# Two-layer hybrid decoder trunk: alternating half-array products, norms by a mean matrix, and a float32 output projection for half of the mixer

## The chip, the cores and the metric

The kernel runs on one core of a Trainium2 chip, as one launch. The metric is device time in microseconds (us). In the profile the engines are PE (TensorE matmuls), PEld (TensorE weight loads), DVE (VectorE), ACT (ScalarE), POOL (GpSimd) and SP (SyncE, which issues most transfers).

## The reference

Two layers act on x (1 x 256 x 1024, float32). Each layer is a half-step SwiGLU feed-forward block, a mixer, and a second half-step SwiGLU block; every one is preceded by an RMS norm and a modulation (shift, scale, gate) that comes from `silu(c) @ ada_w`. The mixer multiplies the normalized x by one matrix of 3088 columns and gives the columns to three groups:

- 8 attention heads of width 64, with normalized and rotated queries and keys, causal over 256 positions (one block, so plain causal attention);
- a convolution group of 256 channels: gate, causal depthwise convolution of 31 taps, a layer norm over each group of 64 channels, silu;
- 4 heads of gated linear attention, in chunks of 64 positions, with a log decay from a rank-16 gate, an RMS norm over each head's 64 values, and a silu gate.

```python
proj = h @ mix_w_in[l]
a_q, a_k, a_v, b_u, c_q, c_k, c_v, c_r, c_g = jnp.split(proj, splits, axis=-1)
o_b = _conformer_conv(b_u, conv_w[l], conv_b[l], conv_norm_g[l], conv_norm_b[l])
log_decay = jax.nn.log_sigmoid(c_g @ gla_gate_w[l] + gla_gate_b[l]) / GLA_TAU
o_c = _merge_heads(_rmsnorm(o_c, gla_out_norm[l])) * jax.nn.silu(c_r)
mixed = jnp.concatenate([o_a, o_b, o_c], axis=-1) @ mix_w_out[l]
x = x + gt2[:, None, :] * mixed
```

## The kernel before

Everything stays on chip, transposed: features on the 128 partitions, the 256 positions along the free axis. x is eight tiles of 128 x 256 (`xT`).

**Products with weights.** Each weight piece of 1 MB is fetched to a `raw` buffer (five of them, `fetch`), and `split` makes two float32r tiles of it: ACT casts a high part `wh` (L328) and DVE subtracts it for a low part `wl` (L331). The other operand is split in the same way (`hT`, `g`, `mix`). A product is then three float32r matmuls, high by high, high by low and low by high (L350 to L352, L356 and L357, L707 to L709, and in the output projection L959 to L961). The small products of the mixer, and the transposes, are float32 without a split, in banks named `tp`.

**The mixer** (`mix`). Its line of work is: convolution inputs first (the 31 taps, L741, then run on DVE between other work), the gate product (L775, L781), then q, k and v in three projections of 512 columns. `attend` is called for four pairs of heads: scores (L838; one head of the pair lies on partitions 0 to 63, the other on 64 to 127), masked maximum on DVE (L845), exponent on ACT, reciprocal of the sum on DVE (L855), scaling on ACT, three transposes on PE (L860), a copy, and the products with v (L865, L866; each head writes one half of the output's partitions). Between the pairs lie the projections of the linear attention. Its own small products are pA (L900, masked into `acaus` by DVE at L905), pS (L916), the running state S on DVE (L921, L926), and pO (L933 with `acaus`, L938 with S).

**The group norms.** `group_rstd` serves the linear attention's output and the convolution's: sums of squares by a matmul with a two-column matrix `grp` (L667), so that the result is 128 x 8; the reciprocal root on that small tile (`rsqrt`: L372, L377 to L386), and eight matmuls with the identity that spread each column over 64 partitions (L674). The convolution also subtracts a mean, which a matmul with the block matrix `grpb` gives (L746).

**The output projection** runs over four pieces of two 128-row blocks, in the order 0, 2 (attention), 6 (linear attention), 4 (convolution). The outputs of all three groups are split (`split_out`, L679 and L680) and multiplied as above.

**What sets the order.** A tile scheduler orders the instructions of each engine before the run, from the program's order, its dependencies and its buffers. At run time every engine works through its own list in that fixed order, and waits on semaphores. The modulation (`ada`, L225 on PE or L234 on DVE, summed at L253 and transposed at L265) is spread over the rest.

Of the kernel before, what the change touches and what calls it, by code (L numbers as in the profile page):

```python
# [17 lines left out]
P = 128  # L18
# [41 lines left out]
def trunk_kernel(ctx: ExitStack, tc: tile.TileContext, x, c, positions, ada_w, ada_b, ffn1_norm, ffn1_w_in,  # L60
# [43 lines left out]
    POOL.memset(epsc, EPS)  # L104
    hpi = keep([P, 1], F32, "hpi")
    POOL.memset(hpi, 1.5707963267948966)

    grp = keep([P, 2], F32, "grp")
    POOL.memset(grp, 0.0)
    POOL.memset(grp[0:64, 0:1], 1.0 / 64)  # L110
    POOL.memset(grp[64:128, 1:2], 1.0 / 64)
# [48 lines left out]
    gatew = keep([32, T], F32, "gatew")  # L160
# [48 lines left out]
    def ada_steps(l):  # L209


        for m0, n in ada_groups(l):
            width = 32 * n
            per = 16 // n
            acc = part = None
            for k in range(KD):
                if k % per == 0:
                    raw = ada_ahead.pop(0) if ada_ahead else next(ada_raws)
                w = raw[:, k % per]
                if ada_mode[0] == "pe":  # L220
                    first = acc is None
                    if first:
                        acc = bank()
                    for q in range(4):
                        PE.matmul(acc[32 * q:32 * q + 32, 0:width], cact[:, k, :], w[:, q, :], start=first,  # L225
                                  stop=(k == KD - 1 and part is None), tile_position=(0, 32 * q))
# [78 lines left out]


# [7 lines left out]
    def split(src, shape, fine=False, raw=None, between=lambda n: None):  # L314
# [23 lines left out]

        state["piece"] += 1
# [6 lines left out]
        return view(hs), view(ls)  # L346
# [336 lines left out]
    def mix(l, done):  # L683
# [31 lines left out]
        for j in range(2):  # L715
            nc.sync.dma_start(gatew[16 * j:16 * j + 16, :], gla_gate_w[l])
# [14 lines left out]
        def conv_steps():  # L731

            y = tv
            for k in range(CK):
                for t in range(2):
                    w = cw[l][:, 2 * k + t:2 * k + t + 1]
                    if k == 0:
                        DVE.tensor_scalar(y[:, t, :], hpad[:, t, 0:T], w, cols[l][:, R_CB + t:R_CB + t + 1],
                                          op0=ALU.mult, op1=ALU.add)
                    else:  # L740
                        DVE.scalar_tensor_tensor(y[:, t, :], hpad[:, t, k:k + T], w, y[:, t, :], op0=ALU.mult,  # L741
                                                 op1=ALU.add)
                yield
            pm = bank()
            for t in range(2):
                PE.matmul(pm[:, T * t:T * t + T], grpb, y[:, t, :], start=True, stop=True)  # L746
            DVE.tensor_sub(y, y, pm.rearrange("p (a b) -> p a b", a=2))
# [23 lines left out]
        ACT.copy(wgs[:, :, 0:16], wg[:, :, 16:32])  # L771
        DVE.tensor_sub(wgs[:, :, 16:32], wg[:, :, 16:32], f32(wgs[:, :, 0:16]))
# [3 lines left out]
        cg = tg[0:32, 0, :]  # L776
        ACT.copy(cg, pp[0:32, T:2 * T])
        DVE.tensor_add(cg, pp[0:32, 0:T], cg)
        pu = bank()
        for t in range(2):  # L780
            PE.matmul(pu[:, T * t:T * t + T], gatew[:, P * t:P * t + P], cg, start=True, stop=True)  # L781
        u, e = unit([P, 2, T], F32, "gu"), unit([P, 2, T], F32, "ge")
        for t in range(2):
            ACT.activation(u[:, t, :], pu[:, T * t:T * t + T], AF.Identity, bias=cols[l][:, R_GB + t:R_GB + t + 1])
# [47 lines left out]
        def attend(pr):  # L832

            ss = [bank(), bank()]
            for i, (qh, kh) in enumerate(((0, 0), (1, 0), (1, 1))):
                for s in range(2):
                    ps = slice(64 * s, 64 * s + 64)
                    PE.matmul(ss[s][:, P * i:P * i + P], qkT[qh][ps, pr, :], qkT[2 + kh][ps, pr, :], start=True,  # L838
                              stop=True)
# [23 lines left out]
            for s in range(2):  # L863
# [33 lines left out]
        for t in range(2):  # L897
            for h in range(2):
                for s in range(2):
                    PE.matmul(pA[s][:, P * (2 * t + h):P * (2 * t + h) + P],  # L900
                              kt[64 * s:64 * s + 64, t, P * h:P * h + P], qt[64 * s:64 * s + 64, t, P * h:P * h + P],
                              start=True, stop=True)
# [8 lines left out]
        for n in range(3):  # L911
            par, h = n % 2, n // 2
            for t in range(2):
                for s in range(2):
                    o = 128 * h + 64 * t
                    PE.matmul(pS[par][64 * s:64 * s + 64, o:o + 64],  # L916
                              ken[64 * par:64 * par + 64, 2 * t + h, 64 * s:64 * s + 64],
                              cv[64 * par:64 * par + 64, h, 128 * t + 64 * s:128 * t + 64 * s + 64],
                              start=True, stop=True)
# [9 lines left out]
        for s in range(2):  # L929
            ps = slice(64 * s, 64 * s + 64)  # L930
            for t in range(2):
                for h in range(2):
                    PE.matmul(pO[ps, T * t + P * h:T * t + P * h + P],  # L933
                              cv[:, h, 128 * t + 64 * s:128 * t + 64 * s + 64], acaus[s][:, 2 * t + h, :],
                              start=(t + h == 0), stop=False)
            for t in range(2):
                for n in range(1, 4):
                    PE.matmul(pO[ps, T * t + 64 * n:T * t + 64 * n + 64], S[ps, n - 1, t, :],  # L938
                              qt[ps, t, 64 * n:64 * n + 64], start=False, stop=(t == 1 and n == 3))
# [17 lines left out]
        def add(d, k, i, wh, wl, first, last):  # L957
            o, cs = tile_of(d), (P * d, P * d + P)
            PE.matmul(o, wh(i, *cs), mixT[k][:, 0:T], start=first and d % 2 == 0, stop=False)  # L959
            PE.matmul(o, wh(i, *cs), mixT[k][:, T:2 * T], start=False, stop=False)  # L960
            PE.matmul(o, wl(i, *cs), mixT[k][:, 0:T], start=False, stop=last and d % 2 == 1)  # L961

        for n, k0 in enumerate(ORDER):
# [3 lines left out]
            wh, wl = split(wo[:, k0:k0 + 2, :], [2, D])  # L967
            if n < 3:
                for i in range(2):
                    for d in range(KD):  # L970
                        add(d, k0 + i, i, wh, wl, n + i == 0, False)
            else:
                for d2 in range(0, KD, 2):
                    for i in range(2):
                        for d in (d2, d2 + 1):
                            add(d, k0 + i, i, wh, wl, False, i == 1)
# [221 lines left out]
```

## Time and profile before

| what | value |
|---|---|
| median of 3 runs | 1063.2 us (1061.58 to 1063.5) |
| the profiled execution's own time | 1062.68 us |
| its span, first to last instruction | 1061.0 us |
| PE busy | 1046.3 us, 99% |
| DVE busy | 855.6 us, 81% |
| ACT busy | 599.8 us, 57% |
| 16 DMA engines, hardware queue q1 | 69.9% |

In the timeline a row gives the start and the length of a run of equal instructions. A matmul's length contains the way through the array after its last column, which the next matmul does not wait for; so what a matmul costs PE is the distance from its start to the next one's start. A float32 matmul stands as two records (two passes), a float32r matmul or a transpose as one. The form `128*64` is the part of the array that a matmul uses, rows by columns. The mixer of layer 0 takes about 225 to 354 us of the span, that of layer 1 about 740 to 866 us.

### The profile page before, as it was taken

Reading aid. Unit: us, or ns where it says so; the run is one execution under the profiler, and the core shown is the slowest. Engines: PE = TensorE matmul, PEld = TensorE weight load, DVE = VectorE, ACT = ScalarE, POOL = GpSimd, SP = SyncE. Lnnn points to the kernel's source line nnn. Section 1 sums busy time; section 2 is a strip of 40 time slices with the busy share of each in tenths; the row PEclk is TensorE's granted clock in tenths of the full one; section 3 lists DMA queues with packets and bytes.
Section 4 is the critical chain, followed back from the end, with each engine's and each line's share of the span. In section 5 each row is a group of like instructions: output and inputs, shape, how many; then the busy total and the mean of one; then the engine's idle time right before and its main releaser. Section 6 shows DMA issues by size and latency. Waiting matters only on the chain.

```text
span 1061.0 us, 17726 instructions
## 1 busy us (share of the span) xinstructions
PE 1046.3 (99%) x6988; PEld 921.1 (87%) x6988; DVE 855.6 (81%) x1430; ACT 599.8 (57%) x1067; POOL 18.1 (2%) x52
## 2 busy tenths in 40 slices
PE   6999999999999999999999999999999999999998
PEld 5899998898888988888889888888988899888887
DVE  3698788879986899999669998865899789976552
ACT  4555454457664865555457565544767577555541
POOL 5000000000000000000000000000000000000000
PEclk9999999999999999999999999999999999999999
DMA  9999999986317369999776998867343436965430
GB/s 314 368 338 351 316 308 321 332 285 187 113 48 234 125 216 339 359 347 326 241 233 200 318 348 297 285 218 237 122 158 120 160 97 224 316 197 173 159 126 20
DMA packets 177512, 251.37 MB, mean 237 GB/s; under 512 B 7429, under 2 KB 156392, under 8 KB 170260
## 3 DMA queue, kind: packets, MB, share of 16 engines
q1 hardware_dynamic: 176608, 250.04, 69.9%
q8 instruction: 55, 0.90, 0.3%
q0 software_dynamic: 704, 0.15, 0.2%
q14 instruction: 29, 0.24, 0.1%
q10 hardware_dynamic: 116, 0.05, 0.0%
HBM read 249.16 MB, written 1.05 MB: 236 GB/s over the span
## 4 chain that ended last, share of the span: by engine, by line
PE 97%; DMA 1%; DVE 1%; ACT 1%; issue 0%; SPq 0%; ACTq 0%
PE mm L356 36%; PE mm L357 18%; PE mm L350 7%; PE mm L351 7%; PE mm L352 7%; PE mm L708 3%; PE mm L707 2%; PE mm L709 2%; PE mm L961 2%; PE mm L960 2%; PE mm L959 1%; PE tp L225 1%; DMA adaraw<-in_ada_w_dram 1%; PE tp L865 1%; PE tp L253 1%; PE tp L838 1%
## 5 line engine op out<-in xcount | busy, mean ns | idle before, releaser
L331 DVE TENSOR_TENSOR wl<-raw,wh 128x1024 fp32r<-128x1024 f32 (+1 forms) x352 | 392.6, 1129 | 106.1 <-ACT wh L328 99.9
L328 ACT CAST wh<-raw 128x1024 fp32r<-128x1024 f32 (+1 forms) x352 | 339.2, 975 | 196.6 <-PE mm L356 102.3
L356 PE MATMUL mm<-hT,wh 128*128 128x512 f32 x912 | 322.6, 397 | 0.0
L357 PE MATMUL mm<-hT,wl 128*128 128x256 f32 x912 | 256.1, 281 | 0.0
L356 PE MATMUL mm<-g,wh 128*128 128x512 f32 x704 | 249.4, 398 | 0.0
L356 PEld LDWEIGHTS mm<-hT,wh 128*128 128x128 f32 x912 | 172.3, 189 | 43.1 <-DVE wl L331 0.8
L357 PE MATMUL mm<-g,wl 128*128 128x256 f32 x704 | 197.6, 281 | 0.0
L350 PE MATMUL mm<-hT,wh 128*128 128x256 f32 (+1 forms) x656 | 187.7, 287 | 2.0 <-ACT wh L328 1.6
L351 PE MATMUL mm<-hT,wh 128*128 128x256 f32 (+1 forms) x656 | 187.6, 286 | 0.0
L352 PE MATMUL mm<-hT,wl 128*128 128x256 f32 (+1 forms) x656 | 186.6, 285 | 0.0
L357 PEld LDWEIGHTS mm<-hT,wl 128*128 128x128 f32 x912 | 171.7, 188 | 0.2
L356 PEld LDWEIGHTS mm<-g,wh 128*128 128x128 f32 x704 | 132.2, 188 | 34.9 <-issue 1.7
L357 PEld LDWEIGHTS mm<-g,wl 128*128 128x128 f32 x704 | 133.0, 189 | 0.0
L350 PEld LDWEIGHTS mm<-hT,wh 128*128 128x128 f32 x656 | 125.0, 191 | 5.4 <-ACT wh L328 2.3
L351 PEld LDWEIGHTS mm<-hT,wh 128*128 128x128 f32 x656 | 125.0, 191 | 1.1 <-DVE hT L436 0.2
L352 PEld LDWEIGHTS mm<-hT,wl 128*128 128x128 f32 x656 | 125.1, 191 | 0.6 <-DVE wl L331 0.2
L234 DVE SCALAR_TENSOR_TENSOR adaacc<-adaraw,cact,adaacc 128x2048 f32<-128x2048 f32 (+1 forms) x59 | 123.5, 2093 | 2.3 <-DMA adaraw<-in_ada_w_dram 2.2
L528 ACT COPY ab<-mm 128x256 f32<-128x256 f32 x114 | 41.5, 370 | 55.5 <-PE mm L357 55.4
L529 DVE TENSOR_TENSOR ab<-ab,mm 128x256 f32<-128x256 f32 x114 | 45.8, 416 | 9.4 <-ACT ab L528 9.1
L534 DVE SCALAR_TENSOR_TENSOR xT<-mm,gate,xT 128x256 f32<-128x256 f32 x80 | 34.5, 477 | 21.0 <-PE mm L357 18.6
L741 DVE SCALAR_TENSOR_TENSOR ab<-hpad,cw,ab 128x256 f32<-128x256 f32 x120 | 50.7, 478 | 0.0
L679 ACT CAST g<-ab 128x256 fp32r<-128x256 f32 x88 | 31.6, 404 | 31.9 <-DVE ab L629 31.0
(226 smaller groups left out, 1123.6 us busy)
## 6 DMA issues: line engine op xcount, KB each, us to landing
raw<-in_ffn_w_in_dram SPq DMA_DIRECT2D x85, 1024.0 KB, 6.2
adaraw<-in_ada_w_dram SPq DMA_DIRECT2D x72, 1024.0 KB, 6.1
raw<-in_ffn_w_out_dram SPq DMA_DIRECT2D x32, 1024.0 KB, 5.8
raw<-in_mix_w_in_dram SPq DMA_DIRECT2D x24, 1024.0 KB, 5.4
raw<-in_ffn_w_out_dram SPq DMA_DIRECT2D x16, 768.0 KB, 5.1
raw<-in_mix_w_out_dram SPq DMA_DIRECT2D x8, 1024.0 KB, 4.8
held<-in_ffn_w_in_dram SPq DMA_DIRECT2D x12, 256.0 KB, 10.6
xn<-in_x_dram SPq DMA_DIRECT2D x2, 512.0 KB, 6.5
```

What stands on the lines that cost most here:

```text
L234: DVE.scalar_tensor_tensor(part, w, cact[:, k, 0:1], part, op0=ALU.mult, op1=ALU.add)
L328: ins = ACT.copy(hs[-1][:, b:c], raw(a + b, a + c)).ins
L331: DVE.tensor_sub(ls[-1][:, b:c], raw(a + b, a + c), f32(hs[-1][:, b:c]))
L350: PE.matmul(o, wh, high, start=first, stop=False)
L351: PE.matmul(o, wh, low, start=False, stop=False)
L352: PE.matmul(o, wl, high, start=False, stop=last)
L356: PE.matmul(halves(o), wh, pair, start=first, stop=False)
L357: PE.matmul(o[:, 0:T], wl, pair[:, 0, :], start=False, stop=last)
L528: ACT.copy(t[:, s, :], o[s][:, T:2 * T])
L529: DVE.tensor_add(t[:, s, :], t[:, s, :], o[s][:, 0:T])
L534: DVE.scalar_tensor_tensor(xT[:, d, :], o, gate[l][i][:, d:d + 1], xT[:, d, :], op0=ALU.mult, op1=ALU.add)
L741: DVE.scalar_tensor_tensor(y[:, t, :], hpad[:, t, k:k + T], w, y[:, t, :], op0=ALU.mult, op1=ALU.add)
```

## The change

1. **Alternation.** Products of two heads, or of two halves, that use different parts of the array are written in turn (second half first), and a helper `row` ties each to the one before in the order of PE's list (order alone, no semaphore): scores, products with v, pA, pS, pO, the gate product (which now uses 32 rows at partition 0 and 32 at partition 32), and the modulation's four products.
2. **Norms.** `group_mean` multiplies by the block matrix `grpb`, so the means come out already spread over the partitions, as 128 x 512; the reciprocal root is taken on that wide tile (four operations on ACT, two on DVE). `grp`, the spreading matmuls and the small tiles go.
3. **Output projection.** The rows of the convolution and of the linear attention (pieces 6 and 4) are used as fetched: `whole` instead of `split`, one float32 matmul instead of three float32r ones, and no split of their operands.
4. The four small transfers of the gate's weights go from SP's queue to POOL's, eight now.

```diff
+    def row(products):
+        for a, b in zip(products, products[1:]):
+            no_sync(b.ins, a.ins, "neighbours")
...
+    def whole(src, shape):
+        raw = fetch(src, shape)
+        piece_done()
+        return lambda k, c0, c1: raw(k * shape[1] + c0, k * shape[1] + c1)
...
-    def group_rstd(sq):
+    def group_mean(y):
         t = bank()
         for tt in range(2):
-            for h in range(2):
-                o = 4 * tt + 2 * h
-                PE.matmul(t[:, o:o + 2], sq[:, tt, P * h:P * h + P], grp, start=True, stop=True)
-        rs = rsqrt(t[:, 0:8], 8, 1.0)
-        bc = bank()
-        for tt in range(2):
-            for h in range(2):
-                o = 4 * tt + 2 * h
-                for s in range(2):
-                    PE.matmul(bc[64 * s:64 * s + 64, T * tt + P * h:T * tt + P * h + P],
-                              rs[:, o + s:o + s + 1].to_broadcast([P, 64]), ident, start=True, stop=True)
-        return bc.rearrange("p (a b) -> p a b", a=2)
+            PE.matmul(t[:, T * tt:T * tt + T], grpb, y[:, tt, :], start=True, stop=True)
+        return halves(t)
+
+    def group_rstd(sq):
+        ms = group_mean(sq)
+        y, v, t = (unit([P, 2, T], F32, "rstd") for _ in range(3))
+        act(y, ms, AF.Ln, bias=epsc)
+        ACT.activation(v, ms, AF.Identity, scale=-0.5, bias=hepsc)
+        act(y, y, AF.Exp, scale=-0.5)
+        ACT.activation(t, y, AF.Square)
+        DVE.tensor_mul(t, t, v)
+        DVE.scalar_tensor_tensor(y, t, 1.5, y, op0=ALU.add, op1=ALU.mult)
+        return y
...
-                split_out(y[:, t, :], mixed(4 + t))
+                mixT[4 + t] = y[:, t, :]
...
-            for s in range(2):
-                ps, vs, pt = slice(64 * s, 64 * s + 64), slice(128 * pr + 64 * s, 128 * pr + 64 * s + 64), tmp[2 + s]
-                PE.matmul(po[ps, 0:T], va[0][:, vs], pt[:, 0:256], start=True, stop=False)
-                PE.matmul(po[ps, P:T], va[1][:, vs], pt[:, 256:384], start=False, stop=True)
+            products = []
+            for h, (a, b) in enumerate(((0, 256), (256, 384))):
+                for s in (1, 0):
+                    ps, vs = slice(64 * s, 64 * s + 64), slice(128 * pr + 64 * s, 128 * pr + 64 * s + 64)
+                    products.append(PE.matmul(po[ps, P * h:T], va[h][:, vs], tmp[2 + s][:, a:b], start=h == 0,
+                                              stop=h == 1))
+            row(products)
...
-            split_out(oc[:, t, :], mixed(6 + t))
+            mixT[6 + t] = oc[:, t, :]
...
+            if k >= 4:
+                PE.matmul(o, w(i, *cs), mixT[k], start=first and d % 2 == 0, stop=last and d % 2 == 1)
+            else:
+                wh, wl = w
...
-            wh, wl = split(wo[:, k0:k0 + 2, :], [2, D])
+            w = (whole if k0 >= 4 else split)(wo[:, k0:k0 + 2, :], [2, D])
```

The lists of the engines change as follows. On PE, layer 0, around the last pair of heads (tmp, va: its softmax and v; cv, gu: pS; acaus and S: pO) the list before was this, with thirteen products of the output projection left out ahead of L933:

```order
L865 MATMUL tp_3609<-tmp_2881,va_2887 64x256
L860 MATMUL tp_3604<-ident_70,tmp_2880 128x128 x2
L866 MATMUL tp_3609<-tmp_2881,va_2888 64x128
L916 MATMUL tp_3625<-cv_3482,gu_2864 64x64 x5
L865 MATMUL tp_3609<-tmp_2882,va_2887 64x256
L866 MATMUL tp_3609<-tmp_2882,va_2888 64x128
L916 MATMUL tp_3626<-cv_3482,gu_2864 64x64 x4
L916 MATMUL tp_3625<-cv_3482,gu_2864 64x64 x3
...
L933 MATMUL tp_3645<-acaus_3551,cv_3482 64x128 x4
L938 MATMUL tp_3645<-qt_3363,S_3639 64x64 x6
L933 MATMUL tp_3645<-acaus_3552,cv_3482 64x128 x4
L938 MATMUL tp_3645<-qt_3363,S_3639 64x64 x6
```

The same place on PE's list now, with the same names:

```order
L882 MATMUL tp_3612<-tmp_2885,va_2890 64x256
L882 MATMUL tp_3612<-tmp_2884,va_2890 64x256
L882 MATMUL tp_3612<-tmp_2885,va_2891 64x128
L882 MATMUL tp_3612<-tmp_2884,va_2891 64x128
L932 MATMUL tp_3629<-cv_3485,gu_2867 64x64 x2
...
L947 MATMUL tp_3648<-acaus_3555,cv_3485 64x128
L947 MATMUL tp_3648<-acaus_3554,cv_3485 64x128
...
L950 MATMUL tp_3648<-qt_3366,S_3642 64x64 x4
L979 MATMUL mm_3727<-mix_3474,wl_3790 128x256
L950 MATMUL tp_3648<-qt_3366,S_3642 64x64 x8
```

The two heads' products with v, which stood apart, are neighbours now, and behind both heads' softmax; pO's two halves alternate, and fewer changes of form lie between them.

On DVE, layer 0, ahead of the last pair's softmax (L845, later L860, whose first operation stands last here), the list before was:

```order
L741 SCALAR_TENSOR_TENSOR ab_2742<-hpad_104,cw_19_115,ab_2742 128x256 x11
L680 TENSOR_TENSOR mix_3471<-tp_3466,mix_3471 128x256
L905 COPY_PREDICATED acaus_3551<-gmask_97,tp_3553 128x512
L741 SCALAR_TENSOR_TENSOR ab_2742<-hpad_104,cw_19_115,ab_2742 128x256
L331 TENSOR_TENSOR wl_3765<-raw_3762,wh_3764 128x1024
L905 COPY_PREDICATED acaus_3552<-gmask_97,tp_3554 128x512
L845 ISA tmp_2879,mx_3575<-tp_3567,amask_89 128x128
```

The same place on DVE's list now (L756 is a tap, L333 the low part of a weight piece, L695 the low part of an attention output, L920 the mask of pA):

```order
L756 SCALAR_TENSOR_TENSOR ab_2742<-hpad_102,cw_19_113,ab_2742 128x256 x6
L333 TENSOR_TENSOR wl_3732<-raw_3729,wh_3731 128x1024
L333 TENSOR_TENSOR wl_3736<-raw_3729,wh_3735 128x1024
L695 TENSOR_TENSOR mix_3474<-tp_3469,mix_3474 128x256
L333 TENSOR_TENSOR wl_3790<-raw_3787,wh_3789 128x1024
L920 COPY_PREDICATED acaus_3554<-gmask_95,tp_3556 128x512
L920 COPY_PREDICATED acaus_3555<-gmask_95,tp_3557 128x512
L860 ISA tmp_2882,mx_3578<-tp_3570,amask_87 128x128
```

Subtractions of weight pieces have moved ahead of the last softmax: from the gate to the mask 16 of them stand on DVE's list in each layer, where 12 (layer 0) and 14 (layer 1) stood, with 54 taps where 53 and 54 stood.

On ACT, the two norms at the mixer's end, layer 0, now (ge and ab: squares; rstd: the wide tiles; mods, sq, hT: work of the next block):

```order
L955 ACTIVATE ge_2868<-tp_3648 128x512
L956 COPY G_2875<-tp_3648 128x512
L330 CAST wh_4112<-raw_4110 128x1024
L384 ACTIVATE rstd_3674<-tp_3671,epsc_77 128x512
L686 ACTIVATE rstd_3675<-tp_3671,hepsc_79 128x512
L384 ACTIVATE rstd_3674<-rstd_3674 128x512
L688 ACTIVATE rstd_3676<-rstd_3674 128x512
L760 ACTIVATE ab_2736<-ab_2742 128x512
L384 ACTIVATE rstd_3712<-tp_3709,epsc_77 128x512
L686 ACTIVATE rstd_3713<-tp_3709,hepsc_79 128x512
L384 ACTIVATE rstd_3712<-rstd_3712 128x512
L381 ACT_TABLE_LOAD
```

Four wide operations stand in each norm's chain where two of 128 x 8 stood, and the second norm's square (L760) stands behind the first norm's chain.

## Rows read from the trace of the kernel before

**Rows 1.** The page: busy time of the engines, PE's granted clock, the chain by engine.
```profile
PE 1046.3 (99%) x6988; PEld 921.1 (87%) x6988; DVE 855.6 (81%) x1430; ACT 599.8 (57%) x1067; POOL 18.1 (2%) x52
...
PEclk9999999999999999999999999999999999999999
...
PE 97%; DMA 1%; DVE 1%; ACT 1%; issue 0%; SPq 0%; ACTq 0%
```

**Rows 2.** Mixer windows: length; PE, PEld, DVE, ACT, POOL busy (instructions); clock, DMA.
```profile
253.00:283.00 30.00, 29.84 (x142) 23.91 (x141) 29.19 (x60) 19.14 (x31) 0.00 (x0) 1.00 0.50 163
283.00:310.00 27.00, 26.97 (x210) 24.02 (x211) 25.00 (x80) 19.92 (x51) 0.00 (x0) 1.00 0.27 93
...
768.00:798.00 30.00, 30.00 (x138) 23.87 (x136) 29.47 (x58) 18.25 (x30) 0.00 (x0) 1.00 0.45 143
798.00:826.00 28.00, 28.00 (x223) 24.50 (x222) 26.46 (x83) 21.78 (x54) 0.00 (x0) 1.00 0.32 111
```

**Rows 3.** PE's timeline, layer 0, third pair and pA: start, length, instruction.
```profile
310.30 0.65 PE L865 MATMUL tp<-tmp,va 128*64 128x256 f32 x2
310.79 0.38 PE L866 MATMUL tp<-tmp,va 128*64 128x128 f32 x2
...
311.47 1.16 PE L900 MATMUL tp<-qt,G 64*128 64x128 f32 x8
312.55 0.39 PE L959 MATMUL mm<-mix,wh 128*128 128x256 f32 x1
312.77 0.28 PE L960 MATMUL mm<-mix,wh 128*128 128x256 f32 x1
312.89 0.28 PE L959 MATMUL mm<-mix,wh 128*128 128x256 f32 x1
```

**Rows 4.** PE's timeline, last pair, pO and norms, layer 0; last row layer 1.
```profile
322.54 0.65 PE L865 MATMUL tp<-tmp,va 128*64 128x256 f32 x2
...
324.33 0.65 PE L865 MATMUL tp<-tmp,va 128*64 128x256 f32 x2
...
326.82 0.52 PE L959 MATMUL mm<-mix,wh 128*128 128x256 f32 x3
327.27 1.09 PE L933 MATMUL tp<-acaus,cv 128*64 128x128 f32 x8
328.29 0.91 PE L938 MATMUL tp<-qt,S 64*64 64x64 f32 x12
329.13 1.09 PE L933 MATMUL tp<-acaus,cv 128*64 128x128 f32 x8
...
331.80 0.99 PE L667 MATMUL tp<-grp,ge 128*128 128x2 f32 x8
...
334.37 1.09 PE L674 MATMUL tp<-ident,rs_o 128*64 128x128 f32 x16
335.39 1.13 PE L746 MATMUL tp<-ab,grpb 128*128 128x256 f32 x4
...
836.70 0.65 PE L865 MATMUL tp<-tmp,va 128*64 128x256 f32 x2
```

**Rows 5.** DVE's timeline: a weight subtraction, the last softmax's start in both layers.
```profile
313.75 1.22 DVE L331 TENSOR_TENSOR wl<-raw,wh 128x1024 fp32r<-128x1024 f32 x1
...
315.49 0.28 DVE L845 CUSTOM_DVE_ANT_0 tmp<-tp,amask 128x128 f32<-128x128 f32 x1
...
343.48 0.69 DVE L750 TENSOR_TENSOR ab<-ab,tp 128x512 f32<-128x512 f32 x1 [1.75 <-PE tp L674]
...
829.87 0.29 DVE L845 CUSTOM_DVE_ANT_0 tmp<-tp,amask 128x128 f32<-128x128 f32 x1
```

**Rows 6.** ACT's timeline at the mixer's end, layer 0: wide, narrow, table load.
```profile
331.09 0.60 ACT L942 ACTIVATE ge<-tp 128x512 f32<-128x512 f32 x1 [3.05 <-PE tp L938]
...
333.03 0.27 ACT L372 ACTIVATE rs_y<-tp,epsc 128x8 f32<-128x8 f32 x1 [0.87 <-DVE rs_v L377]
...
341.15 1.28 ACT L369 ACT_TABLE_LOAD   x1
```

More of the change, by code (lines that the diff above doesn't have):

```diff
@@ L104, in trunk_kernel @@
     POOL.memset(epsc, EPS)
+    hepsc = keep([P, 1], F32, "hepsc")
+    POOL.memset(hepsc, -0.5 * EPS)
     hpi = keep([P, 1], F32, "hpi")
     POOL.memset(hpi, 1.5707963267948966)
[L108 to L111, printed above, removed]
     grpb = keep([P, P], F32, "grpb")
@@ L223, in ada_steps @@
                         acc = bank()
-                    for q in range(4):
-                        PE.matmul(acc[32 * q:32 * q + 32, 0:width], cact[:, k, :], w[:, q, :], start=first,
-                                  stop=(k == KD - 1 and part is None), tile_position=(0, 32 * q))
+                    row([PE.matmul(acc[32 * q:32 * q + 32, 0:width], cact[:, k, :], w[:, q, :], start=first,
+                                   stop=(k == KD - 1 and part is None), tile_position=(0, 32 * q)) for q in range(4)])
                 else:
@@ L714, in mix @@
         nc.sync.dma_start(wg, wi[:, :, 3056:3088])
-        for j in range(2):
-            nc.sync.dma_start(gatew[16 * j:16 * j + 16, :], gla_gate_w[l])
+        for j in range(4):
+            POOL.dma_start(gatew[16 * j:16 * j + 16, :], gla_gate_w[l])
         ws = [split(wi[:, :, c0:c0 + 256], [KD, 256], fine=True) for c0 in (1792, 1536)]
@@ L743, in conv_steps @@
                 yield
[L744 to L747, printed above, removed]
+            DVE.tensor_sub(y, y, group_mean(y))
             ACT.activation(tg, y, AF.Square)
@@ L768, in mix @@
         table("natural_log_exp_and_others")
-        ACT.copy(wgs[:, :, 0:16], wg[:, :, 16:32])
-        DVE.tensor_sub(wgs[:, :, 16:32], wg[:, :, 16:32], f32(wgs[:, :, 0:16]))
+        for j in (0, 32):
+            ACT.copy(wgs[:, :, j:j + 16], wg[:, :, 16:32])
+            DVE.tensor_sub(wgs[:, :, j + 16:j + 32], wg[:, :, 16:32], f32(wgs[:, :, j:j + 16]))
         pp = bank()
@@ L775, in mix @@
             PE.matmul(halves(pp[0:96, :]), wgs[:, k, :], hT[:, k, :, 0:T], start=(k == 0), stop=(k == KD - 1))
[L776 to L781, printed above, removed]
+        cg = tg[0:64, 0, :]
+        ACT.copy(cg, pp[0:64, T:2 * T])
+        DVE.tensor_add(cg, pp[0:64, 0:T], cg)
+        pu = [bank(), bank()]
+        row([PE.matmul(pu[t][:, 0:T], gatew[32 * t:32 * t + 32, P * t:P * t + P], cg[32 * t:32 * t + 32, :], start=True,
+                       stop=True) for t in (1, 0)])
         u, e = unit([P, 2, T], F32, "gu"), unit([P, 2, T], F32, "ge")
         for t in range(2):
-            ACT.activation(u[:, t, :], pu[:, T * t:T * t + T], AF.Identity, bias=cols[l][:, R_GB + t:R_GB + t + 1])
+            ACT.activation(u[:, t, :], pu[t][:, 0:T], AF.Identity, bias=cols[l][:, R_GB + t:R_GB + t + 1])
         ACT.activation(e, u, AF.Abs)
@@ L834, in attend @@
             ss = [bank(), bank()]
+            products = []
             for i, (qh, kh) in enumerate(((0, 0), (1, 0), (1, 1))):
-                for s in range(2):
+                for s in (1, 0):
                     ps = slice(64 * s, 64 * s + 64)
-                    PE.matmul(ss[s][:, P * i:P * i + P], qkT[qh][ps, pr, :], qkT[2 + kh][ps, pr, :], start=True,
-                              stop=True)
+                    products.append(PE.matmul(ss[s][:, P * i:P * i + P], qkT[qh][ps, pr, :], qkT[2 + kh][ps, pr, :],
+                                              start=True, stop=True))
+            row(products)
             for s in range(2):
@@ L862, in attend @@
             po = bank()
-            for s in range(2):
-                ps, vs, pt = slice(64 * s, 64 * s + 64), slice(128 * pr + 64 * s, 128 * pr + 64 * s + 64), tmp[2 + s]
-                PE.matmul(po[ps, 0:T], va[0][:, vs], pt[:, 0:256], start=True, stop=False)
-                PE.matmul(po[ps, P:T], va[1][:, vs], pt[:, 256:384], start=False, stop=True)
+            products = []
+            for h, (a, b) in enumerate(((0, 256), (256, 384))):
+                for s in (1, 0):
+                    ps, vs = slice(64 * s, 64 * s + 64), slice(128 * pr + 64 * s, 128 * pr + 64 * s + 64)
+                    products.append(PE.matmul(po[ps, P * h:T], va[h][:, vs], tmp[2 + s][:, a:b], start=h == 0,
+                                              stop=h == 1))
+            row(products)
             split_out(po[:, 0:T], mixed(pr))
@@ L896, in mix @@
         pA = [bank(), bank()]
[L897 to L902, printed above, removed]
+        row([PE.matmul(pA[s][:, P * (2 * t + h):P * (2 * t + h) + P], kt[64 * s:64 * s + 64, t, P * h:P * h + P],
+                       qt[64 * s:64 * s + 64, t, P * h:P * h + P], start=True, stop=True)
+             for t in range(2) for h in range(2) for s in (1, 0)])
         for s in range(2):
@@ L910, in mix @@
         pS = [bank(), bank()]
-        for n in range(3):
-            par, h = n % 2, n // 2
-            for t in range(2):
+        products = []
+        for t in range(2):
+            for n in (1, 0, 2):
+                par, h = n % 2, n // 2
                 for s in range(2):
                     o = 128 * h + 64 * t
[L916 to L919, printed above, removed]
+                    products.append(PE.matmul(pS[par][64 * s:64 * s + 64, o:o + 64],
+                                              ken[64 * par:64 * par + 64, 2 * t + h, 64 * s:64 * s + 64],
+                                              cv[64 * par:64 * par + 64, h, 128 * t + 64 * s:128 * t + 64 * s + 64],
+                                              start=True, stop=True))
+        row(products)
         S = unit([P, 3, 2, 64], F32, "S")
@@ L928, in mix @@
         pO = bank()
[L929 to L939, printed above, removed]
+        both = [slice(64 * s, 64 * s + 64) for s in (1, 0)]
+        row([PE.matmul(pO[ps, T * t + P * h:T * t + P * h + P], cv[:, h, 128 * t + ps.start:128 * t + ps.stop],
+                       acaus[ps.start // 64][:, 2 * t + h, :], start=(t + h == 0), stop=False)
+             for t in range(2) for h in range(2) for ps in both]
+            + [PE.matmul(pO[ps, T * t + 64 * n:T * t + 64 * n + 64], S[ps, n - 1, t, :], qt[ps, t, 64 * n:64 * n + 64],
+                         start=False, stop=(t == 1 and n == 3))
+               for t in range(2) for n in range(1, 4) for ps in both])
         oc, osq = G.rearrange("p (a c) b -> p a (c b)", a=2), e
@@ L955, in mix, with add @@
         tile_of = lambda d: acc[d // 2][:, T * (d % 2):T * (d % 2) + T]
-        def add(d, k, i, wh, wl, first, last):
+        def add(d, k, i, w, first, last):
             o, cs = tile_of(d), (P * d, P * d + P)
-            PE.matmul(o, wh(i, *cs), mixT[k][:, 0:T], start=first and d % 2 == 0, stop=False)
-            PE.matmul(o, wh(i, *cs), mixT[k][:, T:2 * T], start=False, stop=False)
-            PE.matmul(o, wl(i, *cs), mixT[k][:, 0:T], start=False, stop=last and d % 2 == 1)
+            if k >= 4:
+                PE.matmul(o, w(i, *cs), mixT[k], start=first and d % 2 == 0, stop=last and d % 2 == 1)
+            else:
+                wh, wl = w
+                PE.matmul(o, wh(i, *cs), mixT[k][:, 0:T], start=first and d % 2 == 0, stop=False)
+                PE.matmul(o, wh(i, *cs), mixT[k][:, T:2 * T], start=False, stop=False)
+                PE.matmul(o, wl(i, *cs), mixT[k][:, 0:T], start=False, stop=last and d % 2 == 1)
         for n, k0 in enumerate(ORDER):
```

10 lines of the change are left out of this document (6 added, 4 removed).

## The prediction

> **What bounds the kernel.** I read the page first. PE is busy 99% of the span, the chain that ended last lies on PE for 97%, and the granted clock is 1.00 (2.4 GHz) in every slice [rows 1]. So time is PE's list, and a microsecond taken from it is won unless PE then waits for somebody. Next I cut the mixer into windows, to see who that could be: between the gate and the last pair of heads DVE is busy 29.19 of 30 and 25.00 of 27 us in layer 0, 29.47 of 30 and 26.46 of 28 us in layer 1; ACT has a third of its time free [rows 2]. DVE has 2.8 and 2.1 us to spare there, no more. Last I read PE's timeline, distances from start to start, for what each kind of matmul costs.
>
> **Prices on PE.** A float32r matmul of 256 columns costs 0.12 us (312.77 to 312.89) [rows 3]. A float32 pass of 256 columns costs 0.22: two L865 passes take 0.49 up to L866, 0.05 of it for the change of form [rows 3], and four L746 passes on the whole array take 1.13 with the last one's 0.38 and a change in it [rows 4]. A pass of 128 columns costs 0.11: eight L933 and a change take 1.02 (327.27 to 328.29); one of 64 columns 0.058: twelve L938 and a change take 0.84 (328.29 to 329.13) [rows 4]. Two L667 columns still cost 0.11 a pass [rows 4]. A change of form (128*128 to 128*64 and so on) costs 0.09 where the old form drains (third L959 at 327.06, L933 at 327.27, so 0.21 for 0.12 [rows 4]) and 0.05 to 0.10 at the first instruction of the new one (L959 to L960 0.22 for 0.12 [rows 3]): 0.14 to 0.19; I take 0.15.
>
> Do two halves really run at once? Sixteen L674 passes of 128 columns, which alternate between the column halves in the program, take 1.02 us (334.37 to 335.39); eight L933 of the same form, all in one half, also take 1.02 [rows 4]. They do. The Trainium skill ("TensorE: Matmul & The Clock Gate", Part 3, "What overlaps and what doesn't") says that weight loads overlap running matmuls only when the row group differs. Column halves share their rows, so by that rule the products with v and L933 would gain nothing; the trace disagrees, with the pair of 1.02 beside each other, and I keep that case only as a rival.
>
> **The change, part by part, on PE.**
>
> - Products with v: a head costs 2 x 0.22 + 2 x 0.11 = 0.66; in alternation both heads take one head's time. 8 pairs: -5.3 us.
> - pO: a layer has 16 passes of 0.11 and 24 of 0.058, 3.15 us, in which nothing alternates; half goes. -3.2 for both layers.
> - pA's first half stood alone (8 L900, 0.90 without changes [rows 3]): -0.45 a layer; the gate's four passes of 0.22: -0.44; pS is paired already in part: -0.2. Together -2.2. The scores already alternate.
> - Norms: a call had eight L667 (0.90) and sixteen L674 in pairs (0.93), and now has two products with `grpb`, four passes of 0.22: -0.95, four calls: -3.8.
> - Output projection: 64 products of two passes replace 64 times three float32r matmuls: 0.44 - 0.36 = +0.08 each, +5.1. No row has a float32 product with changing weights of this size on the whole array. Nearest below is 0.12 a pass (-7.7 in all), nearest above 0.27, the L865 pass with its change of form (+11.5). I take 0.22, from L746, which has the same form and width and loads weights for each pass too.
> - Changes of form: 125 in the trace's 6,988 matmuls, 86 counted in the list after (products with v no longer apart, pO in one group, L674 gone). 39 x 0.15 = -5.9 (at 0.14 to 0.19: -5.5 to -7.4).
>
> PE's own work: -5.3 - 3.2 - 2.2 - 3.8 + 5.1 - 5.9 = -15.3 us. The eight `wl` subtractions of 1.22 us [rows 5], their casts and the split outputs that vanish lay beside PE, and count only below. The gate's eight transfers on POOL are issued far ahead of their use; SP loses four: nothing. Raw pieces 6 and 4 now hold their buffers until PE has used them, but the next weight pieces were fetched into the other three.
>
> The Trainium skill ("TensorEngine Tiling (Array Packing)", "Restrictions and Gotchas", Gotcha 1) says that different row tiles cannot access one PSUM bank at a time. L950 now alternates two row tiles that write one bank, which no row before does. By the rule its 24 passes would not pair: 0.7 us a layer back, 1.4 in all.
>
> **What comes back.** First place: the last pair of heads. From the mixer's first product to that pair's first product with v PE's list saves three pairs (-2.0), the gate (-0.4), pA (-0.45) and, counted in the lists, four changes of form in layer 0 (-0.6) and seven in layer 1 (-1.05). Work that moved ahead takes part of it back: two transposes and three float32r products in layer 0 (+0.6), two and ten in layer 1 (+1.4), and in layer 0 two groups of the modulation, sixteen passes of 512 columns, four at a time at twice 0.22 if its four quarters run like the halves (+1.7). Net -1.1 and -2.5. But DVE's list has four (layer 0) and two (layer 1) more `wl` of 1.2 us and one tap more in front of that softmax, against 2.8 and 2.1 us of room [rows 2], part of which is waits for ACT that stay. So I have DVE start this softmax at the same moment as before in layer 0 (315.5) and 1.0 us later in layer 1 (830.9) [rows 5]. From there to both heads' products I add up 8.2 us (two maxima, exponents, reciprocal behind a `wl`, scaling, the second reciprocal behind five half `wl`, transposes, copy); before, the second head's came 8.84 after (315.49 to 324.33 [rows 4, 5]). So the products can start at 323.7 and 839.1. PE would be there at 322.54 - 1.1 = 321.4 and 836.70 - 2.5 = 834.2 [rows 4]. Wait: 2.3 and 4.9, together 7.2 us. Behind L882 PE's whole list waits; nothing passes it. Bounds: 0 to 6 a layer.
>
> Second place: the mixer's end. A narrow step of a norm took 0.2 to 0.27 us, a wide one takes 0.60 on ACT [rows 6] and 0.69 on DVE [rows 5], 128 x 512 both. From the mean of squares to the linear attention's output: four on ACT at some 0.55 apart, three wide ones on DVE and half of the last, about 5 us. PE has under it the two mean products of the convolution, 24 float32r products and four transposes, 5.1 us: 0.2 late. The convolution's chain adds a table load of 1.28 [rows 6], a `wl` of 1.2 and a silu, 7.7 us; under it lie sixteen float32 products of 0.44, 7.0, and 0.8 more: just covered. If the next block's mean square, 28 products behind the end, comes 0.4 late behind its residuals, 0.6 us a layer are lost, 1.2 in all. Bounds: 0 to 2 a layer.
>
> Sum: -15.3 + 7.2 + 1.2 = -6.9. The profiled execution took 1062.7 (median of the runs 1063.2): **1055.8 us**.
>
> **Rivals.**
>
> 1. PE alone decides. DVE's taps can wait, and its idle time is larger than the windows say. Then -15.3: 1047.4. For it: PE is the chain almost throughout. Against: DVE's order is fixed, and `wl` has moved forward. 0.17.
> 2. The wide norms end late in both layers: each chain's steps run one behind the other (0.6 and 0.69 without overlap) and behind casts, 2 us more a layer: 1059.8. For it: sixteen more wide operations on ACT, and the second square stands behind the first chain. Against: 7 us of float32 products cover the longer chain. 0.12.
> 3. Halves don't pair where two moving operands differ (L674 shared one): the 5.3 and the 1.8 of L933 are lost. Of these 7.1, three pairs a layer lie ahead of the wait and only shorten it, 4.0; the other 3.1 come on top: 1058.9. Against: the pair of 1.02. 0.09.
> 4. Slower: the float32 product's weight load is not hidden. Its pass costs 0.22 plus 0.11 (what the 2-column L667 costs, where nothing but the load is left), 128 passes x 0.11 = +14.1, all behind the wait: 1069.9. It decides from +6.9/128 = 0.054 a pass, so above 0.27. For it: no row has a float32 product with changing weights of this width on the whole array. Against: L746 loads for each pass and shows 0.22. 0.07.
>
> That the lists are not what they say is excluded, since they are fixed before the run.
>
> **How the numbers follow.** The forecast's own case holds 0.55 (1050.5 to 1061.5), the rivals 0.17, 0.12, 0.09 and 0.07. The range 1047 to 1060.5 takes in the forecast but for its upper edge, rival 3, most of rivals 1 and 2, leaves out rival 4, and covers waits from nearly 0 to 13 us. A measurement of this kernel tells about 0.2% (2.1 us) from no change. Faster, so under 1061.1: 0.54 + 0.17 + 0.08 + 0.06 = 0.85. Same: 0.01 of the forecast's case, 0.03 each of rivals 2 and 3: 0.07. Slower: rival 4 and the last 0.01 of rival 2: 0.08.
>
> **What would show it.** L882 in pairs a few ns apart, four passes in 0.7 us; L947 and L950 likewise (L950 not, if the bank rule holds); L974 at 0.43 to 0.44 us a product, 13.9 us a layer where 11.5 stood; 86 changes of form. PE idle before the last L882, released by ACT's copy of the softmax, about 2 us in layer 0 and 5 in layer 1, DVE without a gap before it. Small gaps before the first L974 and the next mean square. Wrong it would be if L974 costs over 0.27 a pass, if L882 doesn't pair, or if PE's idle time in the mixers sums to under 3 or over 13 us.

## The result, and the profile after

| | kernel before | changed kernel |
|---|---|---|
| median | 1062.4 us (4 runs) | 1054.1 us (4 runs, 1053.3 to 1056.3) |
| ratio | 1 | 0.9925, 95% interval 0.9913 to 0.9937 |
| profiled execution, its span | 1062.7, 1061.0 | 1054.1, 1052.4 |

Forecast: 1055.8. The time is 1.7 below that and 0.7% faster than before. The page of the changed kernel (lines as in [rows 1]):

```profile
PE 1033.0 (98%) x6844; PEld 908.9 (86%) x6844; DVE 848.7 (81%) x1408; ACT 597.7 (57%) x1061; POOL 21.8 (2%) x58
...
PEclk9999999999999999999999999999999999999999
...
PE 90%; ACT 3%; DVE 3%; DMA 3%; issue 0%; SPq 0%
```

The chain now leaves PE for a tenth of the span. PE's timeline, layer 0 (start, length, instruction, wait and releaser; the place of [rows 4]):

```profile
311.43 1.16 PE L915 MATMUL tp<-qt,G 64*128 64x128 f32 x16
312.43 0.94 PE L852 MATMUL tp<-qkT,qkT 64*128 64x128 f32 x12
...
318.67 0.33 PE L875 MATMUL tp<-ident,tmp 128*128 128x128 f32 x1 [1.03 <-ACT tmp L872]
...
322.83 0.87 PE L882 MATMUL tp<-tmp,va 128*64 128x256 f32 x8
323.63 0.69 PE L932 MATMUL tp<-cv,gu 64*64 64x64 f32 x24
324.26 1.09 PE L947 MATMUL tp<-acaus,cv 128*64 128x128 f32 x16
325.28 0.45 PE L950 MATMUL tp<-qt,S 64*64 64x64 f32 x8
...
325.98 0.68 PE L950 MATMUL tp<-qt,S 64*64 64x64 f32 x16
326.59 0.39 PE L977 MATMUL mm<-mix,wh 128*128 128x256 f32 x1
...
333.83 7.17 PE L974 MATMUL mm<-G,raw 128*128 128x256 f32 x32 [0.25 <-DVE G L960]
340.84 4.48 PE L974 MATMUL mm<-ab,raw 128*128 128x256 f32 x20
```

Two heads' products with v now take 0.80 (322.83 to 323.63, a change of form included), about what one head's took before. All sixteen L947 passes take 1.02 (324.26 to 325.28), as eight did in [rows 4]. Sixteen L950 take 0.61, so these pair too. Sixteen float32 products take 7.01 (333.83 to 340.84), 0.438 each.

Layer 1 went differently. The same view, and below it windows of that stretch (columns as in [rows 2]):

```profile
815.79 1.53 PE L875 MATMUL tp<-ident,tmp 128*128 128x128 f32 x6 [0.32 <-ACT tmp L872]
818.14 0.87 PE L882 MATMUL tp<-tmp,va 128*64 128x256 f32 x8 [0.81 <-ACT tmp L876]
...
819.98 2.08 PE L915 MATMUL tp<-qt,G 64*128 64x128 f32 x16
...
831.87 0.87 PE L882 MATMUL tp<-tmp,va 128*64 128x256 f32 x8
...
843.26 7.17 PE L974 MATMUL mm<-G,raw 128*128 128x256 f32 x32 [1.61 <-DVE G L960]
```

```profile
814.00:818.00 4.00, 2.86 (x19) 1.94 (x17) 4.00 (x13) 4.00 (x14) 0.00 (x0) 1.00 0.00 2
818.00:822.00 4.00, 3.86 (x30) 3.21 (x32) 3.81 (x5) 2.11 (x6) 0.00 (x0) 0.61 0.10 20
822.00:826.00 4.00, 4.00 (x40) 3.88 (x37) 3.82 (x16) 1.62 (x5) 0.00 (x0) 0.96 0.73 247
```

From 815.5 to 818.1, at the end of the third pair's softmax, PE has nothing but six transposes (DVE and ACT are full in that window). Behind that the granted clock falls to 0.5 (1.2 GHz) for some 3.4 us: sixteen L915 passes take 1.87 there (819.98 to 821.85) and 1.00 in layer 0 (311.43 to 312.43). The tenths of the page hide this, since a slice is 26 us long. By windows of 2 us the fall costs 1.6 us. It belongs to the profiled execution: 3.4 us at half speed lower the mean clock of the span by 0.0016, and that execution has 0.998, while the other three have 0.999 and 1.000 and took 1053.3 to 1056.3. So not every execution has this fall, and among these four it does not show in the time. The last pair waits for nobody; the first product behind the linear attention's norm waits 1.61.

### The profile page after: what moved, and what is told of

The parts are those of the page before. It is cut to its first block, busy times and chain, and to the rows that moved or that the text cites. A ratio compares the mean times of both kernels' runs of the same rounds, so it can differ in the third digit from the quotient of the medians.

```text
span 1052.4 us, 17429 instructions
## 1 busy us (share of the span) xinstructions
PE 1033.0 (98%) x6844; PEld 908.9 (86%) x6844; DVE 848.7 (81%) x1408; ACT 597.7 (57%) x1061; POOL 21.8 (2%) x58
## 4 chain that ended last, share of the span: by engine, by line
PE 90%; ACT 3%; DVE 3%; DMA 3%; issue 0%; SPq 0%
PE mm L368 36%; PE mm L369 18%; PE mm L362 7%; PE mm L363 7%; PE mm L364 7%; PE mm L974 3%; PE mm L724 2%; PE mm L723 2%; PE mm L722 2%; DMA held<-in_ffn_w_in_dram 1%; ACT wh L330 1%; DMA adaraw<-in_ada_w_dram 1%; PE tp L222 1%; DVE wl L333 1%; PE tp L250 1%; DVE ab L756 1%
## 5 line engine op out<-in xcount | busy, mean ns | idle before, releaser
L333 DVE TENSOR_TENSOR wl<-raw,wh 128x1024 fp32r<-128x1024 f32 (+1 forms) x344 | 384.0, 1128 | 111.6 <-ACT wh L330 105.5
L330 ACT CAST wh<-raw 128x1024 fp32r<-128x1024 f32 (+1 forms) x344 | 330.9, 973 | 203.7 <-PE mm L368 100.9
L756 DVE SCALAR_TENSOR_TENSOR ab<-hpad,cw,ab 128x256 f32<-128x256 f32 x120 | 51.0, 480 | 0.0
L724 PE MATMUL mm<-wl,hT 128*128 128x512 f32 (+1 forms) x128 | 47.5, 371 | 0.0
```

What stands on the lines that cost most here:

```text
L330: ins = ACT.copy(hs[-1][:, b:c], raw(a + b, a + c)).ins
L333: DVE.tensor_sub(ls[-1][:, b:c], raw(a + b, a + c), f32(hs[-1][:, b:c]))
L724: PE.matmul(pp[t][:, 0:n], a, wl(k, 0, n), start=False, stop=last)
```

## The experiments

Each was timed in five rounds beside the kernel before (e11 and e12 in three). One table first. *List* is PE's own work against before by the prediction's prices, *waits* PE's waits inside the two mixers by the view of waits, *clock* what the lowered clock took, by 2-us windows. Waits and clock are those of the profiled execution, and count gaps above 0.15 us. Before had 0.8 of waits.

| run | list | waits | clock | median | ratio, 95% interval |
|---|---|---|---|---|---|
| changed kernel | -15.3 | 4.9 | 1.6 | 1054.1 | 0.9925 (0.9913-0.9937) |
| e1 alternation alone | -15.4 | 5.0 | 1.6 | 1055.3 | 0.9931 (0.9919-0.9943) |
| e2 norms alone | -5.6 | 9.4 | 3.4 | 1069.2 | 1.0061 (1.0049-1.0074) |
| e3 projection alone | +5.0 | 1.9 | 0 | 1069.1 | 1.0060 (1.0048-1.0072) |
| e4 without projection | -20.3 | 11.6 | 6.8 | 1060.1 | 0.9983 (0.9974-0.9991) |
| e8 all pieces whole | -10.0 | 1.7 | 0 | 1052.9 | 0.9912 (0.9898-0.9925) |
| e9 first piece whole too | -12.1 | 2.3 | 0 | 1052.2 | 0.9905 (0.9891-0.9919) |
| e10 second piece whole too | -12.2 | 4.9 | 1.7 | 1056.4 | 0.9946 (0.9930-0.9961) |

List plus waits (less 0.8) plus clock comes within 2.3 us of the measured change in every row. For the five runs that are not in the table the same sum, with 2.0 for the modulation in e5 and e7, is 1.4 to 2.9 us too low (e6 2.9, e11 2.7), so up to 3 us of a run stay unexplained by it.

**e1, e2, e3: one part each.** e1 has `row` and what it orders, and of the rest nothing:

```diff
+        row([PE.matmul(pA[s][...], kt[...], qt[...], start=True, stop=True)
+             for t in range(2) for h in range(2) for s in (1, 0)])
```

> The kernel before with the alternation alone (row in the scores, products with v, pA, pS, pO, the gate product and the modulation); norms and output projection as before. Theory A (PE's list by the prices of the prediction, plus what PE then waits for): products with v -5.3, pO -3.2, pA, gate and pS -2.2, 31 changes of form fewer at 0.15 = -4.7, so -15.4 on PE; back come the waits on the softmax that the changed kernel's trace shows (1.0 in layer 0, about 2 in layer 1, some 1.6 of lowered clock behind it), so about -10.5: 1052. Theory B (the float32 projection relieves DVE, and without it DVE's subtractions cost PE as much as the projection's longer products): -15.4 + 10 = 1057.

e2 has the wide norms:

```diff
-        rs = rsqrt(t[:, 0:8], 8, 1.0)
+        ms = group_mean(sq)
```

> The kernel before with the norms by a mean matrix alone. Theory A: four calls at -0.95 = -3.8 on PE, 12 changes of form fewer = -1.8, together -5.6; PE waits for the wide norm of the linear attention, 0.25 in layer 0 and 1.6 in layer 1 as in the changed kernel: -3.7, 1058.7. Rival (the wide chain is late in both layers by 2): -1.6, 1060.8.

e3 has the output projection:

```diff
-            split_out(oc[:, t, :], mixed(6 + t))
+            mixT[6 + t] = oc[:, t, :]
```

> The kernel before with the unsplit float32 output projection of conv and linear attention alone. Theory A: 64 products at 0.44 in place of three at 0.12, +5.1, one change of form fewer: +5.0, 1067.4; nothing is won on DVE, since PE waits for nobody before. Theory B: the subtractions and splits that vanish give back what PE pays: +0 to +2, 1062.4 to 1064.4.

e1 came out between its two theories. e3 lies 1.7 above theory A, with a new wait of 1.7 at the norm of layer 1, and far from theory B: DVE's relief alone gives nothing. e2 missed both by 8 us and more, since the wide norm alone makes the kernel slower. Its waits in layer 1:

```profile
PE mm L957 <- ACT mix L680: 5.8, 2, 3.4
```

PE waits for the cast of the split (L680), which stands behind the wide chain, once for each norm; that the float32r products are too short a cover is my reading. The parts sum to -7.3 + 6.6 + 6.5 = +5.8 where all together give -8.3, so they don't add. But the alternation alone already gives -7.3, and its interval (0.9919 to 0.9943) overlaps that of the whole change (0.9913 to 0.9937). Norms and projection cost 6.6 and 6.5 alone; beside the alternation, both together cost nothing, and that they gain anything there is not shown. Alternation and float32 projection with the norms as before were not run.

**e4: the change without the projection.**

```diff
-            mixT[6 + t] = oc[:, t, :]
+            split_out(oc[:, t, :], mixed(6 + t))
```

> The changed kernel without its float32 projection (alternation and norms stay, the projection is split as before). Theory A: the changed kernel less 5.1: 1049.0. Theory B: eight subtractions of 1.22 and the split outputs are back on DVE, and PE waits longer for softmax and norms: 1053 to 1056, no gain.

1060.1, beyond both theories. PE's list is 5 us shorter than the changed kernel's, and the time 6 longer. Layer 0 of e4, PE's timeline and windows:

```profile
340.94 0.28 PE L964 MATMUL mm<-mix,wl 128*128 128x256 f32 x1
343.79 1.01 PE L962 MATMUL mm<-mix,wh 128*128 128x256 f32 x3 [2.58 <-ACT mix L684]
```

```profile
342.00:346.00 4.00, 2.21 (x10) 2.21 (x11) 2.28 (x5) 3.25 (x6) 0.00 (x0) 0.64 0.30 89
346.00:350.00 4.00, 4.00 (x21) 4.00 (x21) 1.13 (x3) 1.52 (x4) 0.00 (x0) 0.51 0.50 173
```

PE stands 2.58 us for the convolution's cast (L684); in the changed kernel, which has no such cast and sixteen products of 0.44 there, that wait is 0. Behind it the clock is at half. So theory B had the right sign and too small a size. Of the 11.6 us of waits 8.7 stand at the casts of the split outputs (L684) and 2.0 at softmaxes in layer 1. e4 takes away three things at once, the cover of the longer products, the missing split and DVE's room, and does not tell what each is worth.

**e5, e6, e7: two repairs.** Fewer taps ahead of the projection's subtractions; half of the norm on DVE; both.

```diff
-TAPS = (4, 2, 4, 4, 4, 4)
+TAPS = (4, 2, 4, 4, 1, 7)
```

```diff
-        ACT.activation(v, ms, AF.Identity, scale=-0.5, bias=hepsc)
+        DVE.tensor_scalar(v, ms, -0.5, -0.5 * EPS, op0=ALU.mult, op1=ALU.add)
```

> The changed kernel with three of the convolution's 31 taps moved from behind the third pair's attention to behind the fourth's (TAPS 4, 2, 4, 4, 1, 7). Theory A (in layer 1 PE has too few products under the third softmax, because the projection weights' subtractions stand behind six taps on DVE): 37 products stand under it in PE's list instead of 29; the wait of about 2 us and the 1.6 that the lowered clock behind it costs go, nine more changes of form cost 1.35: 1051.5 to 1052. Theory B (the chain of softmaxes sets the time, products only move from one wait to the next): the wait comes back at the fourth pair or the norm, 1054 give or take 1.

> The changed kernel with the norm's halved variance (hepsc) computed by DVE beside ACT's logarithm instead of by ACT behind it. Theory A (the first float32 product of layer 1 waits 1.6 us for a norm whose chain runs on ACT): 0.6 of ACT and the convolution's square (0.6) leave the chain in layer 1, 0.25 at most is to be had in layer 0: -1.2 to -1.5, 1052.7. Theory B (DVE's own part of 0.7 takes the same time): 1054.

> The changed kernel with the late taps and the norm's half on DVE together. Theory A: both gains add, 1050.3. Theory B: no gain, 1054.

All three missed: 1059.3 (ratio 0.9968, interval 0.9956 to 0.9980), 1057.2 (0.9952, 0.9939 to 0.9964), 1056.4 (0.9946, 0.9933 to 0.9958). In layer 1 of e5 the clock did not fall and the mixer was 1.1 us shorter, but the waits stayed (3.2 us there, 3.1 in the changed kernel). And the moved taps moved PE's list in layer 0: the modulation's products, four column quarters that run side by side, came apart into more stretches, each of which costs as much as a whole one. PE's timeline of e5:

```profile
307.86 1.05 PE L222 MATMUL tp<-adaraw,cact 128*32 128x512 f32 x2
...
310.63 1.05 PE L222 MATMUL tp<-adaraw,cact 128*32 128x512 f32 x4
...
312.05 1.05 PE L222 MATMUL tp<-adaraw,cact 128*32 128x512 f32 x2
...
313.46 1.05 PE L250 MATMUL tp<-adaacc,ones 128*32 128x512 f32 x2
...
335.78 1.06 PE L250 MATMUL tp<-adaacc,ones 128*32 128x512 f32 x6
338.94 3.32 PE L974 MATMUL mm<-G,raw 128*128 128x256 f32 x8 [2.11 <-DVE G L960]
```

These sixteen passes take five stretches of about 1.0 us, 5.0 in all, where the changed kernel has three and 3.0; behind them PE waits 2.1 for that layer's norm, and the clock falls. `row` fixes an order, not neighbourhood. e6 shows the same kind of trap on DVE (its timeline, layer 1):

```profile
843.36 1.22 DVE L333 TENSOR_TENSOR wl<-raw,wh 128x1024 fp32r<-128x1024 f32 x1
844.50 0.88 DVE L960 SCALAR_TENSOR_TENSOR G<-G,cols,cr 128x256 f32<-128x256 f32 x2
```

A subtraction for the next block now stands in the middle of the norm's chain, ahead of its last step; PE waits 1.93 there, where it waited 1.61, and 1.38 in layer 0, where it waited 0.25. The new operation also started only where ACT's logarithm of the same bank had ended: in the program's order it waits for that.

**e8, e9, e10: more of the projection in float32.** e8 takes all four pieces whole, e9 the first of the two attention pieces, e10 the second:

```diff
-            w = (whole if k0 >= 4 else split)(wo[:, k0:k0 + 2, :], [2, D])
+            w = (whole if k0 in (0, 4, 6) else split)(wo[:, k0:k0 + 2, :], [2, D])
```

> The changed kernel with the attention's half of the output projection in float32 and unsplit too (64 more products). Price alone: 64 times 0.08 = +5.1, 1059.2. Theory A (the projection's longer products pay only where a wait lies beside them): some 2 us of waits under the softmaxes of layer 1 and the clock's 1.6 go, 1055.6 to 1057. Theory B (DVE bounds the mixers): eight subtractions of 1.22 and eight splits less on DVE give more than the price, 1053 or below.

> The changed kernel with the output projection's first piece (pairs 0 and 1 of the heads) in float32 and unsplit too; the second piece stays split. Theory A (the longer products pay where a wait lies beside them, and this piece is what runs under the third and fourth softmax): it keeps what the version with all four pieces whole won in waits and clock, and pays 32 times 0.08 = 2.6 less: 1050.3. Theory B (what won there was DVE's relief by eight subtractions): half of it is back, the wait of layer 1 returns in part, 1053 to 1054.

> The changed kernel with the output projection's second piece (pairs 2 and 3) in float32 and unsplit too; the first stays split. Theory A: the same price on PE, but the products that could run under layer 1's third softmax still wait for their subtractions: its wait (2) and lowered clock (1.6) stay, 1054 to 1056.5. Theory B: same relief of DVE as with the first piece, so the same time as that one within 1.

e8 pays 5.1 us more on PE than the changed kernel and is no slower: theory B's 1053 was met, theory A's 1055.6 too high by 2.7. But e9 and e10 relieve DVE by the same four subtractions and differ by 4.2 us, so theory B falls there. As the traces read, what counts is where the products can run. In e9 the first piece's products need no subtraction and fill the third softmax of layer 1:

```profile
815.45 0.60 PE L978 MATMUL mm<-mix,raw 128*128 128x256 f32 x2
815.88 0.71 PE L875 MATMUL tp<-ident,tmp 128*128 128x128 f32 x5
816.43 1.03 PE L978 MATMUL mm<-mix,raw 128*128 128x256 f32 x4
817.38 0.87 PE L882 MATMUL tp<-tmp,va 128*64 128x256 f32 x8
```

No wait there, no fall of the clock. In e10 they need it, and layer 0 has both, at the last pair:

```profile
319.11 0.47 PE L875 MATMUL tp<-ident,tmp 128*128 128x128 f32 x1 [1.93 <-ACT tmp L872]
```

```profile
318.00:320.00 2.00, 0.89 (x4) 0.89 (x5) 1.24 (x6) 2.00 (x8) 0.00 (x0) 0.79 0.05 7
320.00:322.00 2.00, 2.00 (x10) 1.71 (x9) 0.29 (x1) 1.14 (x3) 0.00 (x0) 0.50 0.95 305
```

So e10's time lies in theory A's range for another reason than its own: layer 1, where it looked for the loss, has no fall and a mixer 1.1 us shorter than the changed kernel's; layer 0's is 4.1 longer.

e9 has the lowest median of all, 2 us under the changed kernel; the intervals of their ratios touch (0.9891 to 0.9919, 0.9913 to 0.9937), and they were not timed beside each other.

**e11, e12: less work on DVE**, in the changed kernel and in the one before.

```diff
-                        DVE.scalar_tensor_tensor(y[:, t, :], hpad[:, t, k:k + T], w, y[:, t, :], ...)
+                        DVE.scalar_tensor_tensor(y[:, t, 0:P], hpad[:, t, k:k + P], w, y[:, t, 0:P], ...)
```

> The changed kernel with 30 of the convolution's 31 taps on half of their columns (half of the convolution is left out): some 12 us less on DVE in each mixer, PE's products unchanged. Theory A (PE waits under the softmaxes because DVE is full): the waits of 1.3 in layer 0 and about 2 in layer 1 and the clock's 1.6 go, 1049. Theory B (the chain through ACT and PE itself sets these waits): 1053 to 1055.

> The kernel before with the same taps halved. PE waits for nobody there, so both theories expect no change, 1061.5 to 1062.5; a gain of several us would mean that DVE held PE already before, which the trace of before does not show.

1058.5 (0.9968, 0.9956 to 0.9979) and 1066.1 (1.0034, 1.0021 to 1.0047): e11 4.4 slower than the changed kernel, e12 3.7 slower than the kernel before, against every expectation. In e11 the waits under the softmaxes are gone, as theory A has it, which speaks for DVE as their cause, though PE's list changed with it. But PE now waits at the norm of both layers:

```profile
PE mm L974 <- DVE G L960: 5.6, 2, 3.0
```

Two things stand behind that. Products that had covered the norm now run earlier: from the linear attention's mean products to L974 PE has 14 float32r products in each layer, where 24 and 17 stood, so the cover is 1.0 and 0.3 us shorter. And the norm's chain is 1.4 and 1.0 us longer, since in both layers a weight subtraction now stands inside it, as in e6. DVE's timeline of e11, layer 1:

```profile
843.61 1.22 DVE L333 TENSOR_TENSOR wl<-raw,wh 128x1024 fp32r<-128x1024 f32 x1
844.75 0.68 DVE L958 TENSOR_TENSOR G<-G,rstd 128x512 f32<-128x512 f32 x1
```

The clock falls behind both of these waits (3.4 us by the windows). e12 has no new wait to speak of; its list has thirteen more changes of form, 2.0 us at 0.15, and where the other 1.7 come from was not settled.

## Why the prediction was right, and where not

**PE's own work: -15.3; shown, a little large.** The span fell by 8.6, with 6.5 of waits and clock that came back and 0.8 that was there before: -14.3. From start to start, both mixers: products with v -6.3 and pO -3.7 (forecast -5.3 and -3.2, there without changes of form); norms -4.4 (-3.8); float32 products 0.438 each (0.44). The scores, put at nothing, took 7.1 where they had taken 8.7, changes of form included: the first pair of layer 0 had not run in halves side by side (1.32 for its twelve passes, now 0.87). The records have 39 changes of form fewer, as counted. The -14.3 is what is left of the span when waits and clock are taken off, not a count of its own.

**Halves pair: right; rival 3 falls.** The Trainium skill's rule on weight loads and row groups ("TensorE: Matmul & The Clock Gate", Part 3, "What overlaps and what doesn't") is not what this trace shows: the two heads' passes start 7 ns apart and share their rows. Nor does the Trainium skill's bank rule ("TensorEngine Tiling (Array Packing)", "Restrictions and Gotchas", Gotcha 1) cost anything here: L950 starts two row tiles into one bank 7 ns apart, and 16 passes took 0.61.

**The float32 weight load is hidden: right; rival 4 falls**, 0.219 a pass (7.01 / 32).

**The last pair: its moment right, the wait's place wrong.** This is the step that failed: "Wait: 2.3 and 4.9", on the last pair. DVE starts the last softmax 62.9 and 63.0 us behind the gate's first product, 62.8 and 62.5 before, so +0.2 and +0.5 (forecast 0 and +1.0):

```profile
314.08 0.28 DVE L860 CUSTOM_DVE_ANT_0 tmp<-tp,amask 128x128 f32<-128x128 f32 x1
...
823.42 0.28 DVE L860 CUSTOM_DVE_ANT_0 tmp<-tp,amask 128x128 f32<-128x128 f32 x1
```

The products came 8.75 and 8.45 later (forecast 8.2). Against the gate they start 1.9 and 2.1 us later than before, where I had 1.2 and 2.4. But PE did not stand in front of them. In layer 0 it waited 1.03 for that softmax, in front of the transposes. In layer 1 the last pair had the projection's products under it, and the waiting had been done at the third pair, 0.32 and 0.81 and gaps between the transposes. I looked for cover at one place, and the list spreads it over four.

**The clock: a term that the sum lacked.** I had waits and not what stands behind them: 1.6 us in layer 1 of the profiled execution.

**The mixer's end: 0.2 right in layer 0 (0.25), wrong in layer 1 (1.61).** I counted one layer's cover for both. Between the linear attention's mean products and its output layer 0 has 24 float32r products and four transposes in PE's list, layer 1 seventeen products, which with the convolution's mean products is 5.2 and 4.2 us of cover; and the chain takes 0.3 longer in layer 1, where ACT squares the convolution in the middle of it (0.63 at 839.36). The loss at the next mean square (0.4 a layer) did not come.

All told 8.4 was to come back and 5.7 did, with 1.0 less saved: the sum is right within 2 us because errors of place cancel. Rival 1 falls by the waits; rival 2 held in layer 1 alone, with 1.4 of its 2 us.

## What to carry to other kernels

When a change takes work off the engine that bounds, list what else runs in each stretch, layer by layer: the saved time returns wherever that engine's list is thin, cover used early is missing later, and work that moves can land inside another chain (e6, e11). A dearer instruction can pay if it needs no preparation and lies beside a wait: the float32 projection costs PE 5 us and saves 6 on balance beside the wide norms (e4 against the changed kernel), but loses 6.5 alone (e3). Time each part by itself before crediting the whole: here the alternation alone gives all of the gain that the intervals can tell. Price a wait of TensorE with the lowered clock that may come behind it, and look for it in windows of 2 us, not in the page's slices.

## What the hardware showed unexpectedly

- Before every fall of the clock in the mixers PE had stood or nearly stood (1.93 in e10, 2.58 in e4, the thin stretch at 815 in the changed kernel). It went to 0.5, and cost 1.6 to 1.7 us (3.4 in layer 0 of e4). Behind the 1.61 at 843.26 of the changed kernel, behind the 1.93 of e6's layer 1 and behind the second wait of e2's layer 1 (2.4), it did not fall: not every wait has this price. Nor does every execution: in e5 those with a mean clock of 0.997 took 1059.1 to 1061.0, those with 0.999 took 1057.6 and 1058.1; in e10 it was 1056.8 to 1060.1 at 0.997 and 0.998, and 1054.0 to 1055.9 at 0.999 and 1.000.
- Less work on DVE made two kernels slower by 4 us (e11, e12): through the order of both lists in e11, in part through more changes of form on PE in e12, where 1.7 stay open.
